# Value pages of the decode in place of dummy products in two seams of a hybrid decoder step, and the fourth tile squared ahead of scaling

## The chip, the core and the metric

The kernel runs on one core of a Trainium2 chip. Its engines work side by side, each through its own list of instructions in a fixed order: TensorE (PE) does matrix products into PSUM, VectorE (DVE) and ScalarE (ACT) do elementwise work and reductions, GpSimd (POOL) does small elementwise work and issues gathering transfers, SyncE (SP) issues the other transfers. Semaphores tie the lists together. The metric is the device time of one execution in microseconds (us).

## The reference, cut to what matters

One layer of a decoder. A prompt of 1024 rows goes through projections, attention with forgetting gates, a gating branch, an output projection, cross-attention to 256 memory rows and a gated MLP. Eight samples of one row each go through the same layer, and their attention runs over 8192 cached rows each, gathered in pages:

```python
xp = xp + merge_heads(fox_prompt(q, k, v, logf), sgu_prompt(u, z, w_s[l], b_s[l]), g_att_out[l], g_sgu_out[l], w_o[l])
xp = xp + cross_attend(rmsnorm(xp, g_cross[l]), mk, mv, w_cq[l], w_co[l])
f, conv_p = conv_ffn(rmsnorm(xp, g_ffn[l]), ..., w_up[l], conv_w[l], conv_b[l], w_down[l])
...
att = fox_sample(q, k, v, logf, cache_k[l], cache_v[l], cache_logf[l], page_table)   # 8 samples, 8192 rows each
```

`rmsnorm` divides each row by the root of its mean square and multiplies by a gain. The sample's rows stay apart from the prompt's until the end, so the two can be interleaved freely.

## The kernel before, in words

**Prompt.** The prompt's rows are worked on in two halves of four tiles of 128 rows (`xt[0]` to `xt[3]`, called the first to the fourth tile here). Each half goes through the output projection of attention (`out_proj` with `w_o`), cross-attention (`cross`, which ends in `out_proj` with `w_co`) and the MLP (`ffn`). A product in single precision is made of three products of rounded high and low parts (lines 1081 to 1083, 272 to 274, 280 to 284). A weight tile's high part is made by ACT (line 235) and its low part by DVE (line 236); the parts of an activation are made by ACT (line 238) and DVE (line 239). This making of parts is called a split here.

**The seam.** `out_proj` computes its second half of columns for tile one, for tile two, and then for tiles three and four together. Each result is added to the residual (line 1015, DVE) and squared and summed on ACT (line 230, from `ssq_into`). For the projection with `w_co` the squares give a factor per row (`factor`, lines 1031 and 1032, ACT and POOL), and the tile is scaled by it. Tiles three and four are scaled by `both`: tile three by ACT (line 1044), tile four by DVE (line 1045), each in two halves. `norm_T` then turns the scaled tiles on PE (line 1124), splits them (lines 238, 239), and starts the MLP's first product: with tiles one and two as the first half of its columns (lines 280, 281, 284), and, when tiles three and four have been turned, with these as the second. Between the two, ahead of the first turning of tiles three and four, stand eight dummy products (`fill`, line 1102). Their results are overwritten by the turning. The stretch from the last product of line 1083 to the second half of the MLP's first product is called a seam here. There are two seams of this kind, one for each half of the prompt. The seams from `w_o` into `cross` have no factors and no dummies, but run through the same `out_proj` and `norm_T`.

**Decode.** The eight samples' attention is a generator (`decode`) that the main loop advances beside the prompt's work, at a pace set by a table of microseconds per step. A step gathers one page of keys by an indirect transfer that POOL issues (line 1428), multiplies and reduces it on DVE (lines 1444, 1448), and every second step asks for a pair of value pages (line 1489), whose eight products (line 1495, sixteen rows in the trace) are issued in the step after. All pages share four buffers (`NKV = 4`). While `held[0]` is true the main loop does not advance the decode. Before, `out_proj` sets it behind the residuals of tiles three and four, and `norm_T` clears it at its end.

**What sets the order.** The program is written through a scheduler that lays out each engine's list with a timing model of its own. `tc.high_priority()` lets instructions go ahead of others, and `tc.issue_after(x)` forbids them to be issued before `x` in the list of their engine.

## Time and profile before

| | us |
|---|---|
| median of three runs | 1794.22 |
| lowest and highest run | 1789.2, 1798.22 |
| span of the profiled execution, first to last instruction | 1791.7 |
| PE busy in it | 1735.9 |
| DVE busy | 1399.9 |
| ACT busy | 733.5 |
| POOL busy | 488.3 |

The page gives the span, not a separate time of the profiled execution; the median of the runs is 2.5 us above the span. A row of the timeline reads: start from the span's beginning, duration, engine, line, operation, output tile, input tile, shapes, count, and in brackets the idle time before it with what ended it. In the rows, `wh` and `wl` are the high and low parts of a weight tile, `u` an activation tile, `ba` and `bb` PSUM banks, `kv` a page buffer, `fac` a factor of scaling, `cp` the constants with the identity matrix that turns a tile, `dv` the PSUM tile of the decode's value sums. Matmuls are pipelined, so a row's duration is longer than the step from one to the next; where a step is meant, it is taken from start to start.

### The profile page before, as it was taken

What the parts mean: (1) busy time and instruction counts of PE and PEld (TensorE: products, weight loads), DVE (VectorE), ACT (ScalarE), POOL (GpSimd) and SP (SyncE); (2) the same over time, 40 slices, a digit from 0 to 9 for tenths busy, and PEclk for the clock granted to TensorE, in tenths of its full rate; (3) what the DMA queues carried; (4) which work ended last, traced back from release to release, by engine and by line L of the source; (5) the groups of instructions that cost most, each with busy time, mean ns of one, the idle gap of its engine ahead of it and who ended that gap; (6) DMA issues with size and microseconds to landing.
All of it is one profiled execution on the core that took longest, in us unless ns stands there. A gap on an engine that the chain in (4) does not pass through costs nothing.

```text
span 1791.7 us, 25124 instructions
## 1 busy us (share of the span) xinstructions
PE 1735.9 (97%) x9653; PEld 1285.7 (72%) x9653; DVE 1399.9 (78%) x1733; ACT 733.5 (41%) x1374; POOL 488.3 (27%) x461
## 2 busy tenths in 40 slices
PE   8999999889999999999999999999999999999997
PEld 5787777655677666767777777766666778768875
DVE  4689658989788986989999999898885549855344
ACT  6332355566643635333333244335353233333232
POOL 1252234443222332333322223433322112102110
PEclk9999999999999999999999999999999999999999
DMA  8786798777697975779788788988879587568982
GB/s 291 297 304 226 294 334 319 259 264 244 254 403 279 363 299 224 282 285 345 290 301 313 291 317 311 376 306 346 320 280 350 214 306 249 191 260 297 359 310 80
DMA packets 157074, 521.06 MB, mean 291 GB/s; under 512 B 20874, under 2 KB 40842, under 8 KB 124186
## 3 DMA queue, kind: packets, MB, share of 16 engines
q0 software_dynamic: 57168, 341.14, 50.0%
q1 hardware_dynamic: 92874, 165.73, 26.5%
q10 hardware_dynamic: 6912, 12.59, 1.9%
q8 instruction: 76, 1.25, 0.3%
q14 instruction: 44, 0.36, 0.1%
HBM read 495.47 MB, written 23.93 MB: 290 GB/s over the span
## 4 chain that ended last, share of the span: by engine, by line
PE 53%; issue 9%; DMA 8%; DVE 6%; ACT 2%; POOL 2%; POOLq 0%; DVEq 0%; ACTq 0%; SPq 0%
DMA kv<-cache_v,io 6%; PE ba L272 6%; PE ba L274 6%; PE ba L273 6%; PE dv L1495 4%; PE bb L272 3%; PE bb L273 3%; PE bb L274 3%; PE ba L1063 1%; DVE s L1448 1%; PE ba L1064 1%; PE ba L1065 1%; PE dv L331 1%; DMA kv<-cache_k,io 1%; PE dv L1774 1%
## 5 line engine op out<-in xcount | busy, mean ns | idle before, releaser
L235 ACT ACTIVATE wh<-wr 128x1024 fp32r<-128x1024 f32 (+2 forms) x220 | 228.6, 1044 | 443.3 <-PE ba L273 142.3
L236 DVE TENSOR_TENSOR wl<-wr,wh 128x1024 fp32r<-128x1024 f32 (+2 forms) x220 | 262.7, 1200 | 165.1 <-PE ba L274 57.4
L1428 POOL DMA_INDIRECT kv<-cache_k,io x128 | 186.9, 1460 | 606.8 <-DVE s L1448 327.2
L1444 DVE TENSOR_TENSOR kv<-kv,d 128x1024 f32<-128x1024 f32 (+1 forms) x156 | 258.0, 1681 | 32.6 <-DMA kv<-cache_k,io 32.6
L1448 DVE TENSOR_REDUCE s<-kv 128x16 f32<-128x1024 f32 (+1 forms) x156 | 258.4, 1672 | 0.0
L1489 POOL DMA_INDIRECT kv<-cache_v,io x128 | 160.8, 1256 | 239.4 <-PE dv L1495 155.2
L272 PE MATMUL ba<-u,wh 128*128 128x512 f32 x528 | 209.3, 397 | 0.0
L274 PE MATMUL ba<-u,wl 128*128 128x512 f32 x528 | 209.0, 396 | 0.0
L273 PE MATMUL ba<-u,wh 128*128 128x512 f32 x528 | 208.5, 395 | 0.5 <-DVE u L239 0.5
L272 PE MATMUL ba<-wh,u 128*128 128x512 f32 (+1 forms) x495 | 186.1, 379 | 0.9 <-ACT u L235 0.9
L273 PE MATMUL ba<-wl,u 128*128 128x512 f32 (+1 forms) x495 | 185.1, 375 | 1.3 <-DVE wl L236 1.3
L274 PE MATMUL ba<-wh,u 128*128 128x512 f32 (+1 forms) x495 | 183.4, 375 | 0.0
L1495 PE MATMUL dv<-kv,s 128*32 128x512 f32 x1024 | 127.1, 598 | 1.6 <-DMA kv<-cache_v,io 1.6
L274 PEld LDWEIGHTS ba<-u,wl 128*128 128x128 f32 x528 | 99.2, 188 | 29.0 <-issue 6.5
L272 PEld LDWEIGHTS ba<-u,wh 128*128 128x128 f32 x528 | 99.3, 188 | 26.4 <-issue 4.8
L273 PEld LDWEIGHTS ba<-u,wh 128*128 128x128 f32 x528 | 99.2, 188 | 25.2 <-issue 2.3
L272 PEld LDWEIGHTS ba<-wh,u 128*128 128x128 f32 x495 | 93.0, 188 | 25.0 <-issue 6.5
L272 PE MATMUL bb<-u,wh 128*128 128x512 f32 x272 | 108.7, 400 | 0.0
L274 PE MATMUL bb<-u,wl 128*128 128x512 f32 x272 | 108.0, 398 | 0.0
L273 PE MATMUL bb<-u,wh 128*128 128x512 f32 x272 | 107.9, 397 | 0.0
L273 PEld LDWEIGHTS ba<-wl,u 128*128 128x128 f32 x495 | 93.0, 188 | 20.1 <-DVE wl L236 1.9
L274 PEld LDWEIGHTS ba<-wh,u 128*128 128x128 f32 x495 | 92.9, 188 | 19.5 <-issue 1.6
(454 smaller groups left out, 3310.6 us busy)
## 6 DMA issues: line engine op xcount, KB each, us to landing
wr<-w_up SPq DMA_DIRECT2D x88, 512.0 KB
kv<-w_up POOLq DMA_DIRECT2D x22, 1024.0 KB
wr<-w_down SPq DMA_DIRECT2D x40, 512.0 KB
kv<-w_down POOLq DMA_DIRECT2D x11, 1024.0 KB
wr<-w_in SPq DMA_DIRECT2D x16, 512.0 KB
wr<-w_o SPq DMA_DIRECT2D x16, 512.0 KB
wr<-w_cq SPq DMA_DIRECT2D x16, 512.0 KB
wr<-w_co SPq DMA_DIRECT2D x16, 512.0 KB
```

The costliest lines, as they stand in the source:

```text
L235: nc.scalar.activation(h, src, AF.Copy)
L236: nc.vector.tensor_tensor(l, src, h.bitcast(F32), op=ALU.subtract)
L272: mmul(out, sh, mh, start=(i == 0), stop=False)
L273: mmul(out, sh, ml, start=False, stop=False)
L274: mmul(out, sl, mh, start=False, stop=(i == n - 1))
L331: mmul(ps[32 * j : 32 * j + 32, :w], xT[:, k, :] if nk == 8 else xT[:, k * 8 : k * 8 + 32], raw[:, q, j * w : (j + 1) * w], start=(k == 0) ...
L1063: mmul(pss[i], mh[k][:, tb], wh, start=(k == korder[0]), stop=False)
L1428: nc.gpsimd.indirect_dma_start(kv, None, a["cache_k"], off(kidx[:, b, ch : ch + 1]))
L1444: nc.vector.tensor_tensor(kvv[:, i : i + m, :], kvv[:, i : i + m, :], qb.unsqueeze(1).broadcast_to((P, m, 512)), op=ALU.mult)
L1448: nc.vector.tensor_reduce(s[:, ch * 4 + i : ch * 4 + i + m, :].rearrange("p k h -> p (k h)"), kvv[:, i : i + m, :].rearrange("p k (h d) -> ...
L1489: nc.gpsimd.indirect_dma_start(kv, None, a["cache_v"], off(kidx[:, b, ch : ch + 1]))
L1495: mmul(dv[32 * j : 32 * j + 32, :], s[:, ch * 4 : ch * 4 + 4, :].rearrange("p k h -> p (k h)"), kvv[:, j, :], start=(ch == 1), stop=(ch == ...
```

## The change

`out_proj` sets `held[0]` ahead of the products of tiles three and four rather than behind them, and at that place asks the decode for up to two pairs of value pages ahead of time (`ask_ahead`). In a seam into the MLP, `norm_T` issues the products of these pages (`give_now`) where `fill` stood, each behind the newest PE instruction, and the turning and splitting of tiles three and four may not be issued ahead of them. If there are no pages, `fill` still runs. `both` keeps ACT's scaling of tile three behind the newest instruction of ACT at the last residual, which is the square of tile four. The decode keeps a list of asked pairs instead of a single one, and ends a sample's value sum when its pages have all been given.

```diff
@@ residual
             ssq_into(sq[:, i, n : n + 1], xs_)
+            squared[:] = [newest(ENG.Activation)]
@@ out_proj
-        def both(r2, r3):
+        def both(r2, r3, end):
...
             for c in (slice(0, 512), slice(512, D)):
-                nc.scalar.activation(y2[:, c], xt[2][:, c], AF.Copy, scale=r2)
+                with tc.issue_after(end):
+                    nc.scalar.activation(y2[:, c], xt[2][:, c], AF.Copy, scale=r2)
                 nc.vector.tensor_scalar(y3[:, c], xt[3][:, c], r3, None, op0=ALU.mult)
...
             for group in ((0,), (1,), (2, 3)):
+                if len(group) == 2:
+                    held[0] = True
+                    if burst:
+                        burst[0]()
...
-                held[0] = len(group) == 2
                 yield 5.2
@@ norm_T
                 if late and kk == 0:
-                    fill(tr, hs)
-                with tc.high_priority():
+                    if not (burst and burst[1](2)):
+                        fill(tr, hs)
+                    behind_ = [newest(ENG.PE)]
+                with tc.high_priority(), tc.issue_after(behind_[0]) if late else nullcontext():
@@ decode
+        def ask():
+            vb, i = divmod(asked[0], 8)
+            if i == 0:
+                dv[vb] = DV()
+            two = [(2 * i, KV()), (2 * i + 1, KV())]
+            if i % 2:
+                two.reverse()
+            pend.append((vb, i, [vstep(vb, c, st[vb], dv[vb], kv) for c, kv in two]))
+            asked[0] += 1
+        def give():
+            vb, i, mms = pend.pop(0)
+            mms[1]()
+            mms[0](newest(ENG.PE))
+            if i == 7:
+                vm[vb] = vmask(vb, dv[vb])
+                masked.append(vb)
+        def ask_ahead():
+            while len(pend) < 2 and asked[0] < able[0] and (not pend or asked[0] % 8):
+                ask()
+        def give_now(n):
+            k = 0
+            while pend and k < n:
+                with tc.issue_after(newest(ENG.PE)):
+                    give()
+                k += 1
+            return k
+        burst[:] = [ask_ahead, give_now]
```

**PE in the first seam.** Before, the end of the MLP's first product on tiles one and two (line 284), the dummies (line 1102), and the turning of tiles three and four (line 1124):

```order
L284 MATMUL ba_6304<-u_6339,wh_6301 128x256 x2
L1102 MATMUL ba_6379<-u_6305 128x256
L1124 MATMUL ba_6396<-cp,u_6373 128x128
L1124 MATMUL ba_6414<-cp,u_6373 128x128
L1102 MATMUL ba_6379<-u_6305 128x256
L1102 MATMUL ba_6379<-u_6316 128x256 x2
L1102 MATMUL ba_6379<-u_6327 128x256 x2
L1102 MATMUL ba_6379<-u_6338 128x256 x2
L1124 MATMUL ba_6379<-cp,u_6373 128x128
```

After (line 284 is the same line; 1495 has become 1505 and 1124 has become 1133; `kv` are value pages):

```order
L284 MATMUL ba_6291<-u_6326,wh_6288 128x256 x2
L1505 MATMUL dv_5415<-kv_6197,s_2862 32x512 x4
L1505 MATMUL dv_5415<-kv_6198,s_2862 32x512 x4
L1505 MATMUL dv_5415<-kv_6202,s_2862 32x512 x4
L1505 MATMUL dv_5415<-kv_6201,s_2862 32x512 x4
L1133 MATMUL ba_6366<-cp,u_6360 128x128
L1133 MATMUL bb_6400<-cp,u_6360 128x128
```

Two pairs of pages stand behind the last product of line 284 and ahead of all turning of tiles three and four. The second seam has one pair at the same place. No dummy product is left in the program (8277 PE instructions before, 8261 after).

**ACT in the first seam.** Before, from the square of tile three (line 230 on `u_4762`) to tile four's factor. Line 238 is a split of tiles one and two, line 1044 the scaling of tile three, `u_4764` tile four:

```order
L230 ACTIVATE junk_6274,sqx_5897<-u_4762 128x512
L238 ACTIVATE u_6338<-bb_6340,gp 128x256
L1031 ACTIVATE fac_1257_6279<-sqx_5897,part_5898 128x1
L1044 ACTIVATE u_6373<-u_4762,fac_1257_6279 128x512 x2
L230 ACTIVATE junk_6277,sqx_5897<-u_4764 128x512
L238 ACTIVATE u_6338<-bb_6340,gp 128x256
L1031 ACTIVATE fac_1258_6282<-sqx_5897,part_5898 128x1
```

After (1031 has become 1033, 1044 has become 1047; the square into `ssu` belongs to the gating branch):

```order
L230 ACTIVATE junk_6261,sqx_5897<-u_4762 128x512
L238 ACTIVATE u_6325<-bb_6327,gp 128x256
L1033 ACTIVATE fac_1256_6266<-sqx_5897,part_5898 128x1
L230 ACTIVATE junk_6264,sqx_5897<-u_4764 128x512
L1047 ACTIVATE u_6360<-u_4762,fac_1256_6266 128x512 x2
L1033 ACTIVATE fac_1257_6269<-sqx_5897,part_5898 128x1
L230 ACTIVATE junk_6272,ssu_5131<-u_5806 128x512
L238 ACTIVATE u_6325<-bb_6327,gp 128x256
```

The square of tile four has moved ahead of the scaling of tile three; the last split of tiles one and two stands behind the scaling in both.

**ACT in the second seam.** Before, from the splits of tiles one and two to tile four's factor (`u_9515` is tile three, `u_9517` tile four):

```order
L238 ACTIVATE u_11069<-ba_11071,gp 128x256
L238 ACTIVATE u_11047<-bb_11049,gp 128x256
L238 ACTIVATE u_11058<-ba_11060,gp 128x256
L238 ACTIVATE u_11069<-ba_11071,gp 128x256
L235 ACTIVATE wh_11391<-wr_11388 128x1024
L230 ACTIVATE junk_11018,sqx_10655<-u_9515 128x512
L1031 ACTIVATE fac_2074_11023<-sqx_10655,part_10656 128x1
L1044 ACTIVATE u_11104<-u_9515,fac_2074_11023 128x512 x2
L230 ACTIVATE junk_11021,sqx_10655<-u_9517 128x512
L1031 ACTIVATE fac_2075_11026<-sqx_10655,part_10656 128x1
```

After, with the square of tile three and its factor further ahead (`u_9505` is tile three, `u_9507` tile four):

```order
L235 ACTIVATE wh_11369<-wr_11366 128x1024
L238 ACTIVATE u_11021<-ba_11023,gp 128x256
L238 ACTIVATE u_11043<-ba_11045,gp 128x256
L238 ACTIVATE u_11054<-ba_11056,gp 128x256
L230 ACTIVATE junk_11006,sqx_10645<-u_9507 128x512
L1047 ACTIVATE u_11089<-u_9505,fac_2073_11008 128x512 x2
L238 ACTIVATE u_11032<-bb_11034,gp 128x256
L1033 ACTIVATE fac_2074_11011<-sqx_10645,part_10646 128x1
L238 ACTIVATE u_11043<-ba_11045,gp 128x256
L238 ACTIVATE u_11054<-ba_11056,gp 128x256
```

Three splits of tiles one and two, which stood ahead of the square of tile three, now stand behind the square of tile four and the scaling of tile three.

More of the change, by code (lines that the diff above doesn't have):

```diff
@@ L1094, in out_proj @@
             with tc.high_priority():
-                ys.append(partial(both, factor(2), factor(3)))
+                end = squared[0]
+                ys.append(partial(both, factor(2), factor(3), end))
         return sq
@@ L1528, in decode @@
             b, ch = divmod(g, 16)
-            if ch == VLAG + 1 and 2 <= b < 10:
-                vend(b - 2, vm[b - 2])
+            if masked and not pend:
+                vend(masked[0], vm[masked.pop()])
             if ch == 0 and 1 <= b < 9:
@@ L1545, in decode @@
                     pm[b] = soft_max(b, st[b], dt_[b])
[L1546 to L1559 removed]
+            while pend:
+                give()
+            n, odd = divmod(g - 16 - VLAG, 2)
+            if 0 <= n < 64 and odd and asked[0] <= n:
+                ask()
             yield left
+        if masked:
+            vend(masked[0], vm[masked[0]])
+        burst.clear()
     rows8 = []
```

19 lines of the change are left out of this document (5 added, 14 removed).

## The prediction

> **What bounds the kernel now.** I read the page's busy times first, then the timeline of each engine around the instructions that the change touches, then busy time by stretch, and last the groups and waits of the work that the change delays.
>
> ```profile
> span 1791.7 us, 25124 instructions
> PE 1735.9 (97%) x9653; PEld 1285.7 (72%) x9653; DVE 1399.9 (78%) x1733; ACT 733.5 (41%) x1374; POOL 488.3 (27%) x461
> ```
>
> TensorE is busy for 97%, so the time moves by what is taken from PE or put on it, and by the 1791.7 − 1735.9 = 55.8 us in which it stands. The span is 2.5 us under the runs' median of 1794.22; I make the sum on this span's stretches and apply it to the median.
>
> The change works in two seams, between the last product of the cross-attention's output projection (L1083) and the MLP. Seam 1 is 692.3 to 704.1, seam 2 is 1325.1 to 1335.1 (columns: stretch, length, busy us of PE, PEld, DVE, ACT, POOL with counts, granted PE clock, DMA):
>
> ```profile
> 692.30:704.10 11.80, 8.57 (x54) 7.67 (x52) 6.84 (x16) 7.07 (x18) 2.12 (x3) 0.86 0.87 361
> 1325.10:1335.10 10.00, 7.26 (x55) 6.08 (x54) 8.47 (x20) 7.85 (x19) 1.78 (x3) 1.00 0.99 406
> 696.20:699.60 3.40, 1.25 (x8) 1.06 (x9) 0.62 (x2) 3.25 (x9) 0.63 (x2) 1.00 1.03 429
> 699.60:703.00 3.40, 3.40 (x18) 3.40 (x17) 2.27 (x7) 0.58 (x2) 1.01 (x1) 0.50 0.64 266
> 1327.63:1331.04 3.41, 2.47 (x20) 2.05 (x19) 3.12 (x8) 2.70 (x6) 0.56 (x1) 1.00 1.02 416
> 706.00:1060.00 354.00, 352.69 (x1671) 262.92 (x1670) 330.17 (x303) 121.14 (x185) 99.10 (x74) 1.00 0.79 297
> ```
>
> PE idles 11.80 − 8.57 = 3.2 us in seam 1 and 10.00 − 7.26 = 2.7 us in seam 2. In seam 1 the clock is halved for 3.4 us, right behind a stretch in which PE worked 1.25 of 3.40 us; in seam 2 a stretch with 2.47 of 3.41 was followed by full clock. So the most that the seams can give is small: idle 5.9 us, the dummies, and the halved clock. PE in seam 1, in order of time:
>
> ```profile
> 692.09 0.39 PE L1083 MATMUL ba<-wh,u 128*128 128x512 f32 x1
> 692.32 0.28 PE L280 MATMUL ba<-u,wh 128*128 128x256 f32 x1
> ...
> 697.71 0.33 PE L1124 MATMUL bb<-cp,u 128*128 128x128 f32 x1 [1.70 <-ACT u L1044]
> 698.68 0.39 PE L280 MATMUL ba<-u,wh 128*128 128x256 f32 x1 [0.64 <-ACT u L238]
> ...
> 699.02 1.46 PE L284 MATMUL ba<-u,wh 128*128 128x256 f32 x8
> 700.27 0.41 PE L1102 MATMUL ba<-u 128*128 128x256 f32 x1
> ...
> 700.77 1.84 PE L1102 MATMUL ba<-u 128*128 128x256 f32 x7
> 702.41 1.21 PE L1124 MATMUL ba<-cp,u 128*128 128x128 f32 x7
> ...
> 703.67 0.27 PE L1124 MATMUL bb<-cp,u 128*128 128x128 f32 x1
> 703.78 0.27 PE L1124 MATMUL ba<-cp,u 128*128 128x128 f32 x1
> ...
> 704.07 0.38 PE L280 MATMUL ba<-u,wh 128*128 128x256 f32 x1
> ```
>
> The waits lie **ahead** of the dummies (L1102), not where they stand: the last of the idle ends at 698.68, the dummies run from 700.27.
>
> **The change, part by part.**
>
> *Dummies out, pages in.* Seam 1 loses eight dummies at half clock (700.27 to 702.41, less two transposes, 1.9 us); seam 2 eight at full clock:
>
> ```profile
> 1324.88 0.39 PE L1083 MATMUL bb<-wh,u 128*128 128x512 f32 x1
> ...
> 1330.90 1.11 PE L1102 MATMUL bb<-u 128*128 128x256 f32 x8
> 1331.85 0.27 PE L1124 MATMUL bb<-cp,u 128*128 128x128 f32 x1
> ```
>
> That is 1331.85 − 1330.90 = 0.95 us. And a pair of value pages (L1495), from a place between two other products:
>
> ```profile
> 1307.67 0.40 PE L1083 MATMUL bb<-wh,u 128*128 128x512 f32 x1
> 1308.00 1.92 PE L1495 MATMUL dv<-kv,s 128*32 128x512 f32 x16
> 1309.86 0.50 PE L1082 MATMUL ba<-wl,u 128*128 128x512 f32 x1
> ```
>
> It costs 1309.86 − 1307.67 − 0.23 = 1.96 us (0.23 is the step between products, 692.32 − 692.09). Two pairs come into seam 1, one into seam 2: 3.9 and 1.96 us of work that leaves other places, where PE was full (352.69 of 354 in the first MLP), so it is a credit if the seam grows by less.
>
> *Squaring the fourth tile first, and what now waits.* ACT in seam 1, then DVE:
>
> ```profile
> 692.52 1.06 ACT L235 ACTIVATE wh<-wr 128x1024 fp32r<-128x1024 f32 x1 [0.97 <-PE ba L1083]
> 693.49 0.46 ACT L238 ACTIVATE u<-ba,gp 128x256 fp32r<-128x256 f32 x1
> ...
> 694.98 0.47 ACT L238 ACTIVATE u<-bb,gp 128x256 fp32r<-128x256 f32 x1 [0.43 <-PE bb L1124]
> 695.35 0.29 ACT L1031 ACTIVATE fac<-sqx,part 128x1 f32<-128x1 f32 x1
> 696.32 1.33 ACT L1044 ACTIVATE u<-u,fac 128x512 f32<-128x512 f32 x2 [0.68 <-POOL fac L1032]
> 697.56 0.61 ACT L230 ACTIVATE junk<-u 128x512 bf16<-128x512 f32 x1
> 698.17 0.45 ACT L238 ACTIVATE u<-bb,gp 128x256 fp32r<-128x256 f32 x1
> 698.53 0.28 ACT L1031 ACTIVATE fac<-sqx,part 128x1 f32<-128x1 f32 x1
> 698.71 0.62 ACT L230 ACTIVATE junk<-u 128x512 bf16<-128x512 f32 x1
> ```
>
> ```profile
> 694.05 0.68 DVE L1015 TENSOR_TENSOR u<-ba,u 128x512 f32<-128x512 f32 x1
> ...
> 699.47 0.88 DVE L1045 TENSOR_SCALAR u<-u,fac 128x512 f32<-128x512 f32 x2 [0.33 <-POOL fac L1032]
> 700.27 0.16 DVE L222 TENSOR_SCALAR r4r<-ssu 128x4 f32<-128x4 f32 x1
> ```
>
> Start to start, ACT takes 0.97 (L235), 0.61 (L230, a square), 0.37 (L238, a split), 0.18 (factor), 1.24 (scale of tile three); factor to scale through POOL takes 0.97, factor to DVE's scale 0.94, that scale 0.80. I lay the new orders on these. **Seam 1**, T being the end of the projection (692.32): L235 to 1.17, square three 1.78, split 2.15, factor; the square of tile four waits for its residual (694.05 + 0.68 = T + 2.4), to 3.0; scale 3.1 to 4.4; factor four; the square of another tile 5.15; the last first-half split 5.6; DVE scales tile four 5.3 to 6.1 and only then forms that split's low part, 6.6. PE's last L284 waits for it: 6.7. Now the pages, which come behind it in the fixed order: 10.6; sixteen transposes at 703.78 − 703.67 = 0.11 (1.76): 12.4, against 704.07 − 692.32 = 11.75. The seam grows by 0.7 and holds 3.9 of pages: **−3.2 us at full clock**. The gap from 2.5 to 5.6 stays open and the clock should halve behind it, as it did; 3.4 us at half rate cost 3.4 × 0.5 = 1.7: **−1.5 us**.
>
> **Seam 2** (T = 1325.11): here the order of ACT is worse than before. The splits of the first half used to stand all ahead of square three; now three stand behind the scale of tile three, and that waits for tile four's square. L235 to 1.17, three splits 2.3, square four (residual at 2.4 as in seam 1) 3.05, scale 4.3, split 4.7, factor, two splits 5.6; DVE scales tile four 5.6 to 6.4, low part 6.9, last L284 7.0, pages 9.0, transposes 10.7, against 10.0 before: +0.7 with 1.96 of pages, **−1.3 us at full clock**. But PE, which needs those splits, now stands nearly idle from 0.4 to 4.7, less busy than the 1.25 of 3.40 that halved the clock in seam 1. With the half clock: **+0.4 us**.
>
> [...]
>
> *Longer hold.* The pause of the decode now starts ahead of the third and fourth tiles' products, in four projections: one background step fewer before each seam. Such a step is a page of keys on DVE:
>
> ```profile
> L1444 DVE TENSOR_TENSOR kv<-kv,d 128x1024 f32<-128x1024 f32 (+1 forms) x156 | 258.0, 1681 | 32.6 <-DMA kv<-cache_k,io 32.6
> L1448 DVE TENSOR_REDUCE s<-kv 128x16 f32<-128x1024 f32 (+1 forms) x156 | 258.4, 1672 | 0.0
> ...
>   DVE kv L1444: 32.6, 18
> ```
>
> (258.0 + 258.4) / 128 pages = 4.03 us each. Two of them are pushed into the first MLP, where DVE idles 354 − 330.17 = 23.8 us and PE does not: covered, 0. Uncovered it is 8.1 us.
>
> *Page loads.* Four value loads are issued ahead of the seam on POOL, one in front of tile three's factor; key loads now follow the seam. DVE waited for key pages 32.6 us in 18 waits, 1.8 each: bounds 0 and 3.6 for two seams; I take 0, since such a wait falls in DVE's idle time. On SP some loads of weights change places by one to three; the nearest price of a late load is the same 0 to 1.8 each, and I take 0 for the same reason. The reduction of a finished value batch moves by one step, same count: 0.
>
> *Sum*, half clock in both seams: −1.5 + 0.4 = −1.1 us. 1794.2 − 1.1 = **1793.1 us**.
>
> **Rivals.**
>
> *Full clock in both seams.* −3.2 − 1.3 = −4.5: 1789.7. For it: seam 2 kept its clock before. Against: each new gap (3.1 and over 3 us) is longer than the longest that stood ahead of the halved clock (1.70).
>
> *The pages do fill the gaps.* If value pages came early enough for PE to lose no time, everything goes: idle 5.9, dummies 1.9 + 0.95, and what the halved clock cost nine transposes (1.21 / 7 = 0.17 each instead of 0.11: 0.5): 9.3 us, 1784.9. Against: the order puts the pages behind the last L284.
>
> *DVE becomes the bound, slower than before.* The two key pages that the longer hold pushes into the first MLP find DVE at 93% there. From the point where its busy time in 706 to 1060 nears the whole stretch, the weights' low parts come late and PE waits: at most 8.1 us, 1793.1 + 8.1 = 1801.2; if the second MLP gave the same again, 1809. For it: DVE is the second busiest. Against: 23.8 us of idle.
>
> *The change does nothing there:* if no pages were ready, dummies would still run and the time stays at 1794.2; the program's order shows pages in both seams, so I leave this almost no chance.
>
> **How the numbers follow.** Forecast (−1.1, give or take 3 for the shifted rest of the order) 0.50; full clock 0.20; gaps filled 0.08; DVE bound 0.20; nothing 0.02. No change is what lies within 0.5%, about what a measurement of this kernel can tell (9 us: 1785.2 to 1803.2; the runs of before lie 9 us apart). Faster takes the half of the gaps-filled case and the tail of full clock, 0.10; slower takes over half of the DVE case and some of the unforeseen, 0.15; the rest, 0.75, is the same. The range 1785 to 1802 reaches from the filled gaps to the DVE case.
>
> **What would show it.** Right: no L1102 rows, sixteen plus sixteen rows of pages in seam 1 and sixteen in seam 2, each behind the last L284; PE idle ahead of them of 3 us and more in both seams; a granted clock of 0.50 for 3.4 us in both; DVE busy 330 to 342 us in the stretch of the first MLP with PE full. Wrong: pages running inside the gap, a clock of 1.00 throughout, or PE idle for low parts of weights in an MLP stretch.

## The result, and the profile after

The changed kernel takes 1813.66 us (median, 1810.04 to 1818.18), against 1794.5 us of the kernel before beside it: a ratio of 1.0114 with a 95% interval of 1.0092 to 1.0136, so 1.1% or some 19 us slower. The forecast was 1793.1 us with a range to 1802. The page of the changed kernel's profiled execution (1810.04 us):

```profile
span 1808.3 us, 25102 instructions
PE 1738.9 (96%) x9637; PEld 1287.3 (71%) x9637; DVE 1399.1 (77%) x1731; ACT 734.7 (41%) x1376; POOL 501.9 (28%) x461
```

PE, DVE and ACT are busy for as long as before, to 3 us; POOL is busy for 13.6 us more with the same number of instructions. PE stands for 1808.3 − 1738.9 = 69.4 us instead of 55.8. Where this is shows when both spans are cut at the same places of the program: the first cross-attention, the first seam, the first MLP with the second half's attention behind it, the projection with `w_o`, the seam behind that, the second cross-attention, the second seam, and the rest. (Columns: stretch, length, busy us of PE, PEld, DVE, ACT, POOL with counts, granted PE clock, DMA share, GB/s.) Before:

```profile
547.06:692.09 145.03, 142.89 (x708) 102.16 (x707) 125.35 (x149) 65.09 (x143) 46.88 (x38) 1.00 0.80 303
692.09:704.00 11.91, 8.68 (x53) 7.80 (x52) 7.00 (x15) 6.97 (x18) 2.12 (x3) 0.86 0.87 363
704.00:1143.93 439.93, 437.63 (x2084) 326.41 (x2083) 411.99 (x394) 158.88 (x249) 131.84 (x94) 1.00 0.81 303
1143.93:1170.44 26.51, 26.51 (x127) 19.53 (x125) 21.14 (x26) 11.23 (x24) 6.02 (x3) 1.00 0.86 334
1170.44:1175.39 4.95, 4.95 (x44) 4.91 (x43) 4.95 (x7) 3.12 (x7) 1.10 (x2) 1.00 0.82 273
1175.39:1324.88 149.49, 144.44 (x709) 99.24 (x708) 131.12 (x144) 63.84 (x139) 53.56 (x44) 1.00 0.86 327
1324.88:1334.68 9.80, 7.07 (x53) 5.91 (x52) 8.27 (x19) 7.43 (x18) 2.00 (x3) 1.00 1.02 420
1334.68:1782.40 447.72, 446.80 (x2922) 331.65 (x2920) 257.38 (x385) 147.41 (x264) 70.24 (x98) 1.00 0.71 259
```

After:

```profile
544.15:691.25 147.10, 141.33 (x693) 102.97 (x692) 120.26 (x146) 65.07 (x144) 46.65 (x35) 0.99 0.80 294
691.25:706.67 15.42, 12.23 (x78) 7.44 (x76) 6.58 (x15) 6.21 (x17) 5.62 (x7) 0.78 0.63 229
706.67:1153.11 446.44, 436.61 (x2069) 325.90 (x2068) 413.88 (x394) 157.64 (x247) 139.93 (x94) 1.00 0.81 304
1153.11:1178.47 25.36, 25.36 (x126) 19.52 (x125) 23.03 (x29) 12.45 (x25) 6.58 (x5) 1.00 0.89 333
1178.47:1186.38 7.91, 5.43 (x44) 4.94 (x42) 7.91 (x11) 2.96 (x7) 3.94 (x1) 1.00 0.86 295
1186.38:1337.70 151.32, 147.26 (x710) 101.45 (x709) 129.37 (x141) 64.55 (x143) 51.09 (x43) 0.98 0.87 326
1337.70:1351.03 13.33, 9.99 (x59) 7.06 (x57) 7.45 (x16) 5.28 (x13) 3.40 (x4) 0.74 0.54 197
1351.03:1799.19 448.16, 445.76 (x2909) 331.43 (x2907) 256.83 (x385) 151.09 (x268) 69.45 (x97) 1.00 0.71 258
```

Pages have moved between stretches, so the lengths are set right by the page rows (L1495, after L1505) that each stretch gained or lost, at the prediction's 1.96 / 16 = 0.12 us a row:

| stretch | longer by, us | page rows | longer without the pages, us | forecast |
|---|---|---|---|---|
| up to the first cross-attention (order unchanged) | −2.9 | 0 | −2.9 | 0 |
| first cross-attention | +2.1 | −16 | +4.0 | 0 |
| first seam | +3.5 | +32 | −0.4 | −1.5 |
| first MLP and what follows | +6.5 | −16 | +8.5 | 0 |
| projection `w_o` and its seam | +1.8 | 0 | +1.8 | 0 |
| second cross-attention | +1.8 | 0 | +1.8 | 0 |
| second seam | +3.5 | +16 | +1.6 | +0.4 |
| second MLP to the end | +0.4 | −16 | +2.4 | 0 |

The sum is 16.8 us. The two seams miss their forecast by 1.1 and 1.2 us; 18.5 us are lost in stretches that were forecast at nothing. The first row, where nothing was moved, says how far two single profiles can lie apart: about 3 us in a stretch. Two profiles further down differ by 4.6 us where their programs are the same.

**The seams.** PE in the first seam, from the last first-half products to the turning:

```profile
693.84 0.38 PE L280 MATMUL ba<-u,wh 128*128 128x256 f32 x1 [0.33 <-ACT u L238]
...
697.20 0.58 PE L280 MATMUL ba<-u,wh 128*128 128x256 f32 x1 [2.87 <-ACT u L238]
...
697.80 1.91 PE L284 MATMUL ba<-u,wh 128*128 128x256 f32 x8
699.64 5.41 PE L1505 MATMUL dv<-kv,s 128*32 128x512 f32 x32
704.98 0.33 PE L1133 MATMUL ba<-cp,u 128*128 128x128 f32 x1
```

and the clock windows around it, and in the second seam:

```profile
693.02:696.43 3.41, 0.99 (x7) 0.58 (x5) 1.78 (x4) 3.33 (x10) 0.74 (x2) 1.00 0.82 298
696.43:699.84 3.41, 2.64 (x14) 2.41 (x18) 1.87 (x6) 1.33 (x5) 1.39 (x2) 0.50 0.00 0
699.84:703.26 3.42, 3.42 (x20) 0.79 (x16) 1.15 (x3) 0.00 (x0) 1.01 (x1) 0.50 0.62 236
703.26:706.67 3.41, 3.41 (x36) 1.94 (x24) 0.00 (x0) 0.02 (x1) 2.48 (x3) 1.00 0.91 292
```

```profile
1338.10:1341.50 3.40, 1.07 (x7) 0.66 (x6) 3.40 (x9) 3.38 (x8) 0.61 (x1) 1.00 1.00 386
1341.50:1344.92 3.42, 2.40 (x11) 2.41 (x12) 2.33 (x7) 1.88 (x5) 0.56 (x1) 0.51 0.76 302
1344.92:1348.33 3.41, 3.41 (x17) 1.91 (x20) 0.00 (x0) 0.00 (x0) 0.00 (x0) 0.50 0.01 5
```

The pages run behind the gap, as forecast, and the clock halves behind it, but for two windows and not for one: 696.43 to 703.26 and 1341.50 to 1348.33. So most of the pages run at half rate: the two pairs take 5.41 us, where 3.9 were forecast. Behind a window of 2.64 busy us at half rate the clock stayed at half; behind one that was full (3.42 of 3.42) it came back.

**The first MLP.** DVE, and then PE, at the two places where PE newly waits for a residual on DVE:

```profile
801.65 2.29 DVE L1454 TENSOR_TENSOR kv<-kv,d 128x2048 f32<-128x2048 f32 x1 [6.13 <-DMA kv<-cache_k,io]
803.97 2.29 DVE L1458 TENSOR_REDUCE s<-kv 128x32 f32<-128x2048 f32 x1
806.18 1.28 DVE L1349 TENSOR_TENSOR u<-ba,u 128x512 f32<-128x512 f32 x2
...
919.37 1.23 DVE L1418 TENSOR_TENSOR_SCAN d<-rmask,d 128x512 f32<-128x512 f32 x1 [5.27 <-ACT d L1417]
...
922.30 0.69 DVE L1349 TENSOR_TENSOR u<-bb,u 128x512 f32<-128x512 f32 x1
```

```profile
806.91 0.50 PE L272 MATMUL ba<-wh,u 128*128 128x512 f32 x1 [1.54 <-DVE u L1349]
...
923.04 0.50 PE L272 MATMUL bb<-wh,u 128*128 128x512 f32 x1 [2.84 <-DVE u L1349]
```

DVE stands 6.13 us for a key page and 5.27 us for the gates of the next sample (ACT's L1417, which itself stands 9.52 us for a small gather), with its list in fixed order. Behind the late instruction stands a residual (L1349) that has to read a PSUM bank before PE may write it again. PE waits for the bank, not for the page. These waits come to 4.4 of the 9.8 us that PE stands in this stretch (2.3 before). The other long ones are for a load (`t<-sgn_d`, 2.2) and for value pages (2.0, against 1.3 before).

### The profile page after: what moved, and what is told of

It is laid out like the page before. It is cut to its first block, busy times and chain, and to the rows that moved or that the text cites. A ratio compares the mean times of both kernels' runs of the same rounds, so it can differ in the third digit from the quotient of the medians.

```text
span 1808.3 us, 25102 instructions
## 1 busy us (share of the span) xinstructions
PE 1738.9 (96%) x9637; PEld 1287.3 (71%) x9637; DVE 1399.1 (77%) x1731; ACT 734.7 (41%) x1376; POOL 501.9 (28%) x461
## 4 chain that ended last, share of the span: by engine, by line
PE 50%; issue 11%; DVE 9%; DMA 5%; POOL 3%; ACT 2%; POOLq 0%; DVEq 0%; SPq 0%; ACTq 0%
PE ba L272 6%; PE ba L273 6%; PE ba L274 6%; PE dv L1505 4%; PE bb L272 3%; PE bb L273 3%; PE bb L274 3%; DMA kv<-cache_v,io 2%; DVE kv L1454 2%; DVE s L1458 2%; PE ba L1067 1%; PE ba L1066 1%; PE ba L1068 1%; PE dv L331 1%; PE dv L1814 1%
## 5 line engine op out<-in xcount | busy, mean ns | idle before, releaser
L235 ACT ACTIVATE wh<-wr 128x1024 fp32r<-128x1024 f32 (+2 forms) x220 | 228.8, 1044 | 482.8 <-PE ba L273 163.5
L1438 POOL DMA_INDIRECT kv<-cache_k,io x128 | 178.1, 1392 | 528.4 <-DVE s L1458 270.4
L1499 POOL DMA_INDIRECT kv<-cache_v,io x128 | 180.9, 1413 | 321.2 <-PE dv L1505 160.0
L1505 PE MATMUL dv<-kv,s 128*32 128x512 f32 x1024 | 128.2, 609 | 3.9 <-DMA kv<-cache_v,io 3.9
```

Of the source, the lines that this page charges most:

```text
L235: nc.scalar.activation(h, src, AF.Copy)
L1438: nc.gpsimd.indirect_dma_start(kv, None, a["cache_k"], off(kidx[:, b, ch : ch + 1]))
L1499: nc.gpsimd.indirect_dma_start(kv, None, a["cache_v"], off(kidx[:, b, ch : ch + 1]))
L1505: mmul(dv[32 * j : 32 * j + 32, :], s[:, ch * 4 : ch * 4 + 4, :].rearrange("p k h -> p (k h)"), kvv[:, j, :], start=(ch == 1), stop=(ch == ...
```

## The experiments

The measure in the text, "lost", is PE's idle time in a stretch plus half of its busy time at half clock there, worked out from each trace's PE rows and granted clock, over the same stretches as above:

| kernel | us | ratio to before | interval | 1st cross | 1st seam | 1st MLP | 2nd seam |
|---|---|---|---|---|---|---|---|
| before | | 1 | | 2.1 | 4.9 | 2.3 | 2.7 |
| changed | 1813.66 | 1.0114 | 1.0092 to 1.0136 | 7.5 | 6.2 | 9.8 | 6.2 |
| `square_only` | 1793.87 | 0.9998 | 0.9979 to 1.0017 | 2.5 | 5.1 | 2.1 | 5.1 |
| `no_dummies` | 1792.29 | 1.0005 | 0.9986 to 1.0025 | 6.7 | 4.1 | 2.5 | 3.7 |
| `pause_only` | 1794.80 | 1.0002 | 0.9989 to 1.0016 | 3.0 | 4.3 | 3.0 | 3.6 |
| `pause_square_dummies` | 1801.54 | 1.0050 | 1.0029 to 1.0072 | 2.6 | 4.9 | 3.8 | 5.0 |
| `turning_free` | 1800.88 | 1.0053 | 1.0035 to 1.0072 | 7.1 | 3.9 | 4.6 | 4.0 |
| `ask_only_mlp` | 1817.29 | 1.0147 | 1.0113 to 1.0181 | 2.3 | 4.9 | 15.2 | 5.4 |
| `ask_only_w_o` | 1805.33 | 1.0077 | 1.0055 to 1.0098 | 5.5 | 6.2 | 2.1 | 3.1 |
| `one_pair` | 1804.06 | 1.0072 | 1.0052 to 1.0093 | 11.8 | 5.9 | 3.5 | 5.0 |
| `early_two_pairs` | 1793.53 | 1.0009 | 0.9993 to 1.0024 | 8.3 | 0.3 | 3.6 | 1.1 |
| `early_one_pair` | 1801.93 | 1.0065 | 1.0046 to 1.0085 | 10.9 | 0.8 | 8.1 | 1.9 |
| `early_first_seam` | 1801.12 | 1.0057 | 1.0036 to 1.0077 | 8.2 | 0.3 | 5.1 | 5.0 |
| `early_second_seam` | 1806.31 | 1.0079 | 1.0063 to 1.0095 | 9.8 | 4.9 | 18.2 | 1.1 |
| `early_two_pairs_late_keys` | 1800.03 | 1.0038 | 1.0023 to 1.0054 | 8.1 | 0.0 | 6.2 | 8.7 |
| `early_two_pairs_ask_mlp` | 1791.17 | 0.9991 | 0.9976 to 1.0007 | 2.7 | 0.3 | 4.4 | 6.1 |
| `early_first_rest_before` | 1789.94 | 0.9994 | 0.9983 to 1.0005 | 3.0 | 0.3 | 4.4 | 1.5 |
| `early_asked_sooner` | 1800.06 | 1.0041 | 1.0021 to 1.0060 | 5.5 | 0.4 | 11.7 | 5.1 |

The lost times are of one profile each. Before and `no_dummies` have the same program up to the first seam, and lose 2.1 and 6.7 in the first cross-attention; a difference under 5 us between two such entries says little unless it repeats. The profiled execution need not lie at the median: that of `ask_only_mlp` lies 3.8 us below it, those of `early_second_seam` and `early_two_pairs_late_keys` 5.0 and 4.7 us above. The kernel before was measured again beside each group of kernels (medians 1790.5 to 1794.5 us), so kernels are compared here by their ratios.

### Parts of the change by themselves

**square_only**, on the kernel before:

```diff
+                with tc.issue_after(end):   # end: the square of tile four
                     nc.scalar.activation(y2[:, c], xt[2][:, c], AF.Copy, scale=r2)
```

> The kernel before with one edit: ACT's scale of the third tile may not be issued ahead of the square of the fourth. Pause, dummies and decode as before. By the prediction's working on ACT's order the first half's last split comes later in both seams: 1 to 3 us slower for both seams together, with half clock in the first. Rival (any shift of the order moves waits in the MLP as it moved them in the changed kernel): 6 us or more in either direction, with new waits outside the seams.

No change. PE's order differs in several hundred rows, and the time stays: a shift of the order is not slower as such. Where the pause starts early, the bound has little left to move: in `pause_only`, which lacks it, the square of tile four already stands ahead of the scaling of tile three in both seams.

**no_dummies**, on the kernel before:

```diff
-                if late and kk == 0:
-                    fill(tr, hs)
```

> The kernel before without its dummy products; nothing stands in their place. By the prediction's rows they took 1.9 us (at half clock) in the first seam and 0.95 in the second: 2 to 3 us faster if they only cost their time; if they keep the clock up behind them, a half clock of 3.4 us comes in the second seam (+1.7) and the whole is 1 us faster at most.

The dummies' price cannot be told from nothing: 0.05% slower, the interval reaches from 2.5 us faster to 4.5 us slower. The credit of 1.9 + 0.95 us for them has no support.

**pause_only**, on the kernel before:

```diff
             for group in ((0,), (1,), (2, 3)):
+                if len(group) == 2:
+                    held[0] = True
...
-                held[0] = len(group) == 2
```

> The kernel before with one edit: the pause of the decode starts ahead of the products of the third and fourth tiles in all four projections. No pages are asked, dummies stay, ACT's scale is not bound. Theory that the longer pause is what loses the first MLP (one more key page is pushed there and DVE stands for a page ahead of a residual): 7 us slower than the kernel before or more, with waits of TensorE for DVE's residual L1349 (here some lines earlier) in the first MLP. Rival (the pages in the seam lose it, through the four buffers that they take): within 3 us of the kernel before.

No change: the longer pause is covered, as the prediction had it. The DVE rival, as it was put (two key pages pushed into the MLP), falls.

**pause_square_dummies**, on the changed kernel:

```diff
-        burst[:] = [ask_ahead, give_now]
-        burst.clear()
```

> The changed kernel without asking: no page is asked ahead or given in a seam, so the dummies run in both seams; the earlier pause, the bound on ACT's scale and the bound on the turning behind the dummies stay. Theory that the pages lose the time: 0 to 4 us slower than the kernel before. Rival (the pause and ACT's order lose it): 8 us slower or more, and the second seam keeps its gap of over 3 us.

Some 9 us slower than before by the ratio, with an interval from 5 to 13: the pages are not the whole of it, and the measurement lies at the rival's bound of 8. The second seam's gap is there too (1.16 and 2.18 us in the profile), yet that seam loses only 1.4 us more than with the pause alone. What this kernel has beyond `pause_only` is, beside ACT's bound, the rule that the turning and splitting of tiles three and four may not pass the dummies. Part of the difference turns up in a seam that the rule does not touch, that from `w_o` into the second cross-attention: first `pause_only`, then this kernel,

```profile
1166.04:1171.53 5.49, 5.23 (x44) 4.94 (x43) 5.49 (x7) 3.23 (x7) 1.19 (x2) 1.00 0.94 328
```

```profile
1168.89:1176.80 7.91, 5.43 (x44) 4.94 (x43) 7.91 (x11) 2.96 (x7) 3.94 (x1) 1.00 0.86 295
```

2.4 us longer with DVE busy for all of it, and in the same form as in the changed kernel. That the rule causes it is not shown: `early_two_pairs` below has no such rule and takes 8.44 us there.

**turning_free**, on the changed kernel:

```diff
-                    behind_ = [newest(ENG.PE)]
-                with tc.high_priority(), tc.issue_after(behind_[0]) if late else nullcontext():
+                with tc.high_priority():
```

> The changed kernel without the bound that keeps the turning and splitting of tiles three and four behind the pages. In the first seam the order then puts both pairs behind the whole turning and the second half's first product follows them; in the second seam the pair stays ahead of most of the turning. The same bound behind dummies cost 6.7 us (1801.5 against 1794.8 with the pause alone). Theory that the bound on the turning is a cost by itself: 5 us or more off the changed kernel's 1813.7. Rival (the pages come behind the gap in any case and the keys stay late): within 3 us of the changed kernel.

0.61% or 11 us off the changed kernel by the ratios, though in the first seam the pages now come even later, behind the turning. The bound on the turning, with the order that follows from it, is a large part of the loss.

### Asking ahead

**ask_only_mlp**, on the changed kernel (and **ask_only_w_o** with `ys is None` in its place):

```diff
-                    if burst:
+                    if burst and ys is not None:
                         burst[0]()
```

> The changed kernel, but value pages are asked ahead only in the projection with w_co; in the projection with w_o none are asked, and the earlier pause stays in all four. TensorE's rows differ from the changed kernel's only in the two cross-attentions and the seams ahead of them. Theory of places (each loss belongs to the stretch in which TensorE stands or runs at half clock; in the changed kernel against the kernel before these were +5.4 us in the first cross-attention, +2.5 in the seam into the second, +1.8 in the second, +1.3 in the first seam into the MLP, +7.5 in the first MLP, +3.5 in the second seam, +1.5 behind it): the first three go, about 9.7 us, so about 10 us slower than the kernel before, and the first MLP still loses about 7. Rival (the early pages of w_o cost nothing, their stretches lose by chance): still 18 to 20 us slower than the kernel before.

> The complement of the kernel that asks only ahead of the MLP: pages are asked ahead only in the projection with w_o; pause and bounds as in the changed kernel, dummies where no page is pending. Against the kernel with pause, bounds and dummies (1801.5). Theory of places: the first cross-attention loses 5 us more: 1806 to 1808. Rival (what one stretch loses the next one need not lose): 1800 to 1803.

The first cross-attention is repaired by not asking in `w_o`. Five kernels with an early pause and no asking there have it at 142.1 to 142.8 us; a sixth, `early_asked_sooner`, which pauses and asks one tile sooner at the end of this stretch, has it at 145.0. The seven with two pairs asked in `w_o` have it at 145.5 to 149.4 us, with the same page rows in it. That is 5.0 us in the mean (147.4 against 142.5, without the sixth). But the theory that a repaired stretch shortens the whole falls: for `ask_only_mlp` the ratio should have fallen from 1.0114 to 1.0055, and it is 1.0147, with an interval from 1.0113. Its program for the first seam and the MLP is the changed kernel's row for row, but for the last 40 us, and the MLP lost 15.2 instead of 9.8. Both stretches together lose 17.5, against 17.3 in the changed kernel: what PE gained by arriving 5 us sooner it waited out later. The complement, `ask_only_w_o`, costs 0.27% or 4.8 us more than `pause_square_dummies` by the ratios. That is near the theory's 5, but the intervals overlap, and the place is not the theory's: in the profiles the first cross-attention loses 2.9 us more (5.5 against 2.6) and the second, which also stands behind a projection that asks, 6.9 more (12.6 against 5.7).

### The place and the number of the pages

**early_two_pairs**, on the changed kernel:

```diff
+            if t0 == 0 and callable(ys[2]) and burst:
+                burst[1](2)
             first(hs, ls, c)
...
-                if late and kk == 0:
-                    if not (burst and burst[1](2)):
-                        fill(tr, hs)
-                    behind_ = [newest(ENG.PE)]
-                with tc.high_priority(), tc.issue_after(behind_[0]) if late else nullcontext():
+                with tc.high_priority():
```

> The changed kernel with its pages at another place of the seam: they are given right behind the turning of tiles one and two, ahead of the MLP's first products on these, where TensorE stood for 3 us; nothing is put where the dummies stood. Both pairs are asked ahead as in the changed kernel. Theory of late keys: the buffers come free some 5 us earlier than in the changed kernel, the gap of the seam is filled (idle under 1 us, full clock, 4 to 5 us less in the first seam) and the first MLP loses 3 to 5 instead of 7.5: 8 to 12 us slower than before. Rival (the loss follows from the planned order and not from the keys): seams gain 4 to 8, the MLP still loses 7 or more: 10 to 15 us slower.

The whole loss is gone, which neither theory had: 1793.53 us, 0.09% above the kernel before and not to be told from it. The edit does two things: it moves the pages up, and it takes away the bound on the turning. `turning_free`, without the bound alone, is 0.61% (11 us) below the changed kernel, so 0.44% (8 us) is what the place of the pages adds to that. Windows of the first seam, the first MLP and the second seam:

```profile
691.06:700.53 9.47, 9.16 (x78) 6.11 (x76) 5.09 (x11) 6.65 (x18) 5.63 (x7) 1.00 0.90 330
700.53:1140.78 440.25, 436.60 (x2068) 326.05 (x2067) 412.39 (x396) 157.33 (x247) 139.07 (x93) 1.00 0.81 308
...
1324.83:1333.24 8.41, 7.36 (x57) 5.13 (x56) 7.30 (x16) 5.70 (x14) 3.43 (x4) 1.00 0.98 365
```

PE in the first seam:

```profile
692.49 0.60 PE L1129 MATMUL bb<-cp,u 128*128 128x128 f32 x4
693.02 3.64 PE L1503 MATMUL dv<-kv,s 128*32 128x512 f32 x32
696.59 0.39 PE L280 MATMUL ba<-u,wh 128*128 128x256 f32 x1
```

The same 32 page rows now run at full clock in what was the gap. Stretch by stretch the page rows are the changed kernel's, so lengths compare directly: first seam 9.47 instead of 15.42 us, second 8.41 instead of 13.33, and the first MLP 440.25 instead of 446.44 us, with not one instruction of it edited.

**one_pair** (on the changed kernel) and **early_one_pair** (on `early_two_pairs`):

```diff
-            while len(pend) < 2 and asked[0] < able[0] and (not pend or asked[0] % 8):
+            while len(pend) < 1 and asked[0] < able[0] and (not pend or asked[0] % 8):
```

> The changed kernel, but only one pair of value pages is asked ahead at a time, so that two of the four page buffers stay with the keys through the seam. Theory of late keys (four value pages hold every buffer until their products run in the seam, key loads are issued only behind them, DVE's key work and all that hangs on it runs late through the first MLP, and DVE then stands for a page ahead of a residual that PE needs): the first MLP loses under 2 us instead of 7.5 over the kernel before, and the whole is 6 to 9 us slower than before, near the kernel with pause, square and dummies (8 us). Rival (any value page in the seam shifts the planned order and the MLP loses by that): 15 us slower or more.

> As the one with both pairs given early, but with one pair asked at a time. Theory of late keys: seams filled and the keys in time, 0 to 4 us faster than the kernel before. Rival: the MLP loses 7 or more in spite of it, 5 us slower than before or more.

With one late pair the first MLP loses little (3.5), as the theory of late keys had it; the time is 13 us above before instead of 6 to 9, since the first cross-attention now loses 11.8. With one early pair it should have been the best of all and is 11 to 12 us slower than before: the MLP loses 8.1, the first cross-attention 10.9. That miss goes against the theory.

**early_two_pairs_late_keys**, on `early_two_pairs`:

```diff
+        if late:
+            nc.gpsimd.tensor_copy(sm([P, 4], "lateq", 1), hs[7][:, 508:512].bitcast(F32))
+            latek[:] = [newest(ENG.Pool)]
...
+            with tc.issue_after(latek[0]) if latek else nullcontext():
                 nc.gpsimd.indirect_dma_start(kv, None, a["cache_k"], off(kidx[:, b, ch : ch + 1]))
```

> The kernel with both pairs given early, and one copy of 4 columns added on GpSimd behind the last split of the seam's turning, which no key load may be issued ahead of: the buffers come free as early as there, but the key loads go out only behind the seam, as in the changed kernel. Theory of late keys: the first MLP loses 6 to 9 us instead of 3.6, with DVE standing for key pages ahead of residuals, seam 1 stays filled: 4 to 8 us slower than the kernel with both pairs early. Rival (the first MLP's loss in the changed kernel came from the planned order, not from when the keys are loaded): the first MLP stays at 3 to 4 us of loss.

0.29% or 5 us slower than `early_two_pairs` by the ratios, inside the 4 to 8 of the theory, but not where it said. The first MLP loses 6.2, 2.6 more than without the delay, a difference no larger than chance between two profiles. Most sits around the second seam (8.7 lost, and 157.26 us of second cross-attention instead of 150.16), where PE's order differs too. With `turning_free`, whose keys are as late (the first key load goes out 11.5 us behind the projection, in the changed kernel 10.6) and whose MLP lost 4.6, late key loads do not by themselves explain the changed kernel's first MLP.

**early_first_seam** and **early_second_seam**: the pages early and the turning free of the bound in one seam, both as the change has them in the other (`turns` counts the seams):

```diff
-            if t0 == 0 and callable(ys[2]) and burst:
+            if t0 == 0 and callable(ys[2]) and len(turns) == 1 and burst:   # 2 in the other kernel
```

> The changed kernel with its pages given early (behind the turning of tiles one and two) in the first seam alone; the second seam stays as changed. Up to the second seam the order is that of the kernel with both pairs given early (1793.5). Theory that the pages behind the gap cost each seam its own time and the first seam the MLP's too: seam 1 gains 6, the first MLP 6, so about 12 to 14 us off the changed kernel's excess of 20 over the kernel before: 6 to 8 us slower than before, with the second seam at 6 us of loss. Rival (the MLP's loss is not tied to the pages' place): 12 to 15 us slower than before.

> The changed kernel with its pages given early in the second seam alone; up to there its order is the changed kernel's, row for row. Theory: the first MLP again loses 9 to 10 us (it repeats, being the same program), the second seam gains 5 and the end 1: 13 to 15 us slower than the kernel before. Rival (the first MLP's loss was a matter of that run): under 10 us slower.

These two share the loss out between the seams. By the ratios, early pages with free turning are worth 0.57% (10 us) in the first seam and 0.35% (6 us) in the second, together 0.92%, and 1.05% (19 us) in both, which is the same within the intervals. The first kernel is 10 us slower than before, between the theory's 6 to 8 and the rival's 12 to 15 (the interval, 6 to 14 us, reaches into both), with the first seam at 0.3 us of loss, as the theory had it, and the first MLP at 5.1 instead of 9.8. The second is 14 us slower, as expected. It runs the changed kernel's program up to the second seam, and its first MLP lost again, and more:

```profile
707.31:1161.60 454.29, 440.82 (x2069) 328.68 (x2068) 415.30 (x395) 158.30 (x248) 147.57 (x94) 0.99 0.80 301
```

```profile
921.76 1.22 DVE L1424 TENSOR_TENSOR_SCAN d<-rmask,d 128x512 f32<-128x512 f32 x1 [6.76 <-ACT d L1423]
```

```profile
925.43 0.80 PE L272 MATMUL bb<-wh,u 128*128 128x512 f32 x1 [4.69 <-DVE u L1355]
```

The wait at the gates came again at the same place, with 4.69 us for PE this time; 4.7 of the 18.2 us were lost at half clock. PE stood 5.3 us for value pages as well (2.0 in the changed kernel). So the loss repeats with this order; its size differs from run to run.

What differs at the entry to the MLP is how much DVE gets done. The 40 us behind the projection, DVE's column being the fifth: before, changed, `turning_free`, `early_two_pairs`:

```profile
692.09:732.09 40.00, 36.57 (x192) 29.15 (x191) 30.91 (x41) 19.14 (x40) 6.70 (x7) 0.96 0.63 248
```

```profile
691.25:731.25 40.00, 36.02 (x190) 26.73 (x189) 27.14 (x37) 18.70 (x39) 7.62 (x9) 0.91 0.65 240
```

```profile
689.55:729.55 40.00, 37.68 (x203) 29.60 (x202) 33.21 (x44) 20.63 (x42) 8.59 (x9) 0.96 0.74 280
```

```profile
691.06:731.06 40.00, 38.69 (x214) 30.04 (x213) 31.42 (x41) 21.28 (x43) 7.42 (x9) 1.00 0.72 255
```

And DVE behind its scale of tile four in the changed kernel:

```profile
696.84 0.88 DVE L1048 TENSOR_SCALAR u<-u,fac 128x512 f32<-128x512 f32 x2 [2.04 <-POOL fac L1034]
...
707.16 1.27 DVE L239 SCALAR_TENSOR_TENSOR u<-ba,gp,u 128x256 fp32r<-128x256 f32 x3 [6.17 <-ACT u L238]
```

While the pages run, the turning may not start, its splits have nothing to split, and no key page has come: DVE stands for 6.17 us and does 27.1 us of work instead of 30.9 (27.7 and 28.4 in `ask_only_mlp` and `early_second_seam`). It enters an MLP in which it is busy for 93% with 4 to 6 us of work owed. The three kernels with that order are the three that lose 9.8, 15.2 and 18.2 there; the two above with DVE busy for 31 us and more lose 3.6 and 4.6. This fits, but `early_one_pair` and `early_asked_sooner`, with DVE busy for 32.1 and 32.2 us, lose 8.1 and 11.7 without such a debt, and `one_pair` and `ask_only_w_o`, with DVE busy for only 29.2 and 28.9 of those 40 us, lose 3.5 and 2.1. It is not the whole of it. Which of the two, the debt or the places at which the order puts residuals behind late gathers, carries how much stays open.

### For speed

**early_two_pairs_ask_mlp** joins `early_two_pairs` and the edit of `ask_only_mlp`. **early_first_rest_before** has early pages in the first seam alone, no asking elsewhere, and dummies with free turning in the second seam. **early_asked_sooner** is the first of these with pause and asking started one tile sooner, ahead of tile two:

```diff
+                if group == (1,) and burst and ys is not None:
+                    held[0] = True
+                    burst[0]()
```

> The kernel with both pairs given early in the seam (1793.5 us against 1790.9 of before), but with pages asked ahead only in the projection with w_co. That kernel lost 3.9 us more than the kernel before in the first cross-attention (8.3 us of idle and half clock against 2.1, with a shorter path), 2.9 in the seam into the second. Theory of places: the first cross-attention is back at 2 to 3 us of loss, so 4 to 6 us faster than that kernel: 1786 to 1789, 0.1 to 0.3% faster than before. Rival (what the first cross-attention gains is lost again in the first MLP, as with asking only ahead of the MLP in the changed kernel: 17.3 and 17.5 us of loss over both stretches): no faster than 1793.

> A version for speed: pages asked ahead and given early in the first seam alone; no asking ahead elsewhere; dummies and free turning in the second seam as in the kernel before; the pause early in all four. The kernel with pages early in both seams and asked only ahead of the MLP was 0.9 us faster than before and lost 6.1 us in its second seam to a page that had not landed. Theory: the second seam loses 3 to 4 and the dummies 1, the rest as there: 1788 to 1790, 0.1 to 0.2% faster than before. Rival (stretches pay for one another): no faster than before.

> As the kernel with pages early in both seams and asked only ahead of the MLP, but pause and asking start one tile sooner, ahead of the products of tile two, so that the pages have landed by the second seam. Theory: the wait of 3.0 us for a value page in the second seam goes with its half clock: 3 to 5 us faster than that kernel, 1786 to 1788, if the longer pause stays covered as it was in the kernel with the pause alone. Rival: two key pages fewer are done ahead of each seam and the MLP or the next cross-attention loses them: no faster than 1791.

The first gave back in the second seam, where PE stood 2.97 us for a value page, what it gained in the first cross-attention. The second, 1789.94 us, has the lowest median of all and lies where it was expected, but its interval (0.9983 to 1.0005) holds no change. The third is 7 us slower by the ratio: its first MLP loses 11.7, and why stays open. No version beats the kernel before by more than can be measured.

## Why the prediction was wrong

- **Dummies out.** They left, 16 rows of L1102. The credit for them (1.9 and 0.95 us) was not found when they alone were taken out (a ratio of 1.0005).
- **Seam 1, −1.5 us.** Place and gap were right: pages behind the last L284, PE idle for 2.87 us in one wait ahead of them, DVE's scale of tile four at T + 5.36 (696.84 − 691.48) against 5.3 forecast. The half clock was mis-sized: two windows, not one, and the second over the pages, which took 5.41 us. PE lost 3.0 us to it for the 1.7 of the sum. Measured −0.4.
- **Seam 2, +0.4 us.** Again right in its mechanism (waits of 1.16 and 2.18 us for splits behind the scaling), again two windows at half clock, 2.9 us lost for 1.7. Measured +1.6. The two differences of 1.3 and 1.2 us account for the seams' misses of 1.1 and 1.2.
- **Full clock rival.** It fell. Windows with 0.99 and 1.07 us busy of 3.41 and 3.40, neither of them idle, were followed by half clock. The clock rose behind 3.42 of 3.42 us busy in the first seam and 3.41 of 3.41 in the second; in the kernel before it rose behind a window of 2.97 busy us at half rate (317.28 to 320.69).
- **Gaps filled rival, 1784.9.** The change did not do it, but `early_two_pairs` did: 0.3 and 1.1 us lost in the seams, no half clock. Its seams are worth what the rival said. The time did not follow (1793.53): in its profile the first cross-attention lost 8.3 us (2.1 before) and the seam from `w_o` into the second 2.9 (none before).
- **Longer hold, taken as 0.** Right for the pause alone: a ratio of 1.0002.
- **The step that failed: *Page loads*, taken as 0 "since such a wait falls in DVE's idle time".** The prediction set 23.8 us of idle DVE in the first MLP against late pages and against the work pushed there, and priced both at nothing. The work did fit: DVE was busy for 413.9 us of the whole stretch against 412.0 before. But DVE's waits did not fall where they cost nothing. It stood 6.13 us for a key page and 5.27 us for gates, each time with residuals behind it in fixed order, and PE stood 4.4 us for their banks. In all, the stretch grew by 8.5 us without the page rows; how the other 4 us divide among the remaining waits and DVE's late start stays open. The DVE rival named the place and nearly the price (8.1, at 0.20 of the chance), but the price was luck: its two key pages of the pause cost nothing by themselves, and PE waited for residuals rather than for low parts of weights.
- **A step that was missing:** in the projection with `w_o` two pairs are asked ahead and nothing takes them in its seam. They hold all four buffers until the decode resumes. The prediction costed asking only as page loads in two seams, at 0 to 3.6 us, taken as 0. In the profiles it cost the first cross-attention 5.0 us; the time of the whole kernel did not fall when this asking alone was taken out.
- **And the bound on the turning** was costed inside the seam alone. With the order that follows from it, it is worth 11 us.

## What to carry to other kernels

Filler work belongs where the engine stands, not behind it: the same 48 page rows, moved up by some 6 to 8 us and with nothing held behind them any more, were worth 19 us. In the profiles 11 us of that lie in the seams and the rest in stretches that nobody edited. About 11 of the 19 came already with the free turning, 8 with the place. Idle time of an engine with a fixed order was no cover here for work pushed onto it (DVE stood 6.13 and 5.27 us in the changed kernel's first MLP, and PE 4.4 us behind it); on this evidence it can be one only if the idle time comes after that work is ready and ahead of the instruction that the bounding engine waits for. A bound on order ("behind the newest instruction") should be priced by what the other engines cannot do meanwhile.

## What the runs showed of the hardware

In the changed kernel the granted clock of TensorE fell to 0.50 behind windows that were 29% and 31% busy (0.99 of 3.41 us from 693.02, 1.07 of 3.40 us from 1338.10), and stayed there behind windows of 2.64 and 2.40 us busy at half rate, while 2.47 of 3.41 us busy at full rate (from 1327.63) had kept it full in the kernel before. Two windows at half rate followed in each seam, behind a gap of 2.87 us in the first and gaps of 1.16 and 2.18 us in the second. Other windows of 3.41 us in the trace of the kernel before: at full rate, 1.83 us busy (from 365.07) were followed by half rate and 1.71 us (from 1177.44) by full rate; at half rate, 2.73 us (from 368.48) were followed by another half and 2.97 us (from 317.28) by full rate. So in these windows the clock came back only behind a busier one (2.97 us) than some that had kept it (1.71 and 2.47 us). And the DMA engines moved next to nothing for 3.4 us in each seam of the changed kernel (0.00 busy and 0 GB/s from 696.43, 0.01 and 5 GB/s from 1344.92).
